# Seven block products instead of eight in the feed-forwards of a hybrid trunk

## The chip, the cores and the metric

The kernel runs on one core of a Trainium2 chip. The metric is the device time of one execution in microseconds (us), lower is better. The profiles are single executions taken by the hardware profiler; PE is the tensor engine, PEld its weight loads, DVE the vector engine, ACT the scalar engine, POOL the GpSimd engine, SP the queue that issues the transfers.

## The reference

A trunk of two layers over 512 latent tokens and 256 context tokens, model width 1024. Each layer is a half-step feed-forward, a mixing of the tokens by four groups of heads, and a second half-step feed-forward; every one of them starts from a modulated RMS norm. What matters here:

```python
def swiglu(h, w_in, w_out):            # w_in: 1024 x 5632, w_out: 2816 x 1024
    a, b = jnp.split(h @ w_in, 2, axis=-1)
    return (jax.nn.silu(a) * b) @ w_out

x = x + 0.5 * mx[2][:, None] * swiglu(modulate(x, ...), p['ffn_in'][0], p['ffn_out'][0])
# ... the mixers ...
x = x + 0.5 * mx[8][:, None] * swiglu(modulate(x, ...), p['ffn_in'][1], p['ffn_out'][1])
```

The context goes through the same weights, but not in the last feed-forward, whose result nobody reads.

## The kernel before

Everything is feature-major: features on the 128 partitions, tokens along the free axis (768, or 512 in the last feed-forward). The two streams are held side by side, so a feed-forward is one matrix product over 768 columns. There are four feed-forwards, called F1 to F4 here: F1 and F3 begin the two layers, F2 and F4 end them. F4 has 512 tokens, the others 768.

Products are kept near float32 accuracy by splitting each operand into a high part, rounded to the format that the tensor engine takes, and a low part, the rest (`split`, L72 to L78: ACT casts the high part at L77, DVE or POOL subtracts for the low part at L78). One product is then three matmuls: high by high, high by low, low by high.

`ffn` (L308) walks over 22 feature tiles in four parts (`PARTS`, 6, 6, 5 and 5 tiles). For a tile, `weights` loads 128 x 2048 weights (8 blocks of input features by 256 output features, the gate's 128 and the value's 128) and splits them; `x_ffn_in` makes the two products, for the first 512 tokens and then for the other 256 (two times 256 in F4), takes the silu of the first, multiplies, and splits the result into `g`. The first two tiles of a feed-forward are done together, segment by segment, since the second segment's norm is still under way. After a part, `out_product` multiplies the part's rows of the second weight matrix and adds to `X` (`resid`, L276). The last part's second product runs segment by segment (`out_and_norm`), so that the norm of the first segment runs beside the products of the second.

Work on the side: the modulation of later sub-layers (`mod_tile`, L179) is given to `ffn` as a list of calls, three or two for each tile. A modulation tile is one load of 512 KB and two multiply-and-accumulate operations of DVE over 128 x 1024 (L186). F1 has 56 of these tiles, F2 24, F3 48, F4 none.

The order of the work of each engine is not written by hand: a planner puts each instruction on its engine's queue by its own estimate of when it is ready, in the order of the program where several are. Each engine then runs its queue strictly in order.

Of the kernel before, what the change touches and what calls it, by code (L numbers as in the profile page):

```python
# [17 lines left out]
L = 2  # L18
# [6 lines left out]
PARTS = (6, 6, 5, 5)  # L25
# [3 lines left out]
# columns of the packed per-partition vectors  # L29
# [17 lines left out]
# feature tiles of the input projection: R = rwkv, then the others  # L47
# [5 lines left out]
class Net:  # L53
# [4 lines left out]
    # ---------------------------------------------------------------- small helpers  # L58
# [29 lines left out]
    def rsqrt(self, pool, val, n, cap=None, tag=""):  # L88
        """1/sqrt of [128, n] values in SBUF"""
# [15 lines left out]
    # ---------------------------------------------------------------- constants  # L105
# [20 lines left out]
    # ---------------------------------------------------------------- phase of dense layers  # L126
    def open_early(self, st):
        """what the output projection needs; attention still runs"""
# [3 lines left out]
        self.wp = p(name="wp", bufs=2)  # L132
# [19 lines left out]
    def weights(self, src, nk, w, pool=None, hi_eng=None):  # L152
        """load [128, nk, w] and split it"""
        pool = pool or self.wp
        raw = pool.tile([128, nk, w], F32, tag="wraw", name="wraw", bufs=2 if pool is self.wp else 3)
        hi = pool.tile([128, nk, w], F32R, tag="whi", name="whi")
        lo = pool.tile([128, nk, w], F32R, tag="wlo", name="wlo")
        self.load(raw, src)
        self.split(hi, lo, raw, None if pool is self.wp else self.nc.gpsimd, hi_eng)
        return hi, lo  # L160

    def product(self, w, sl, h, sg, nk):
        """rows sl of the weights times the tokens sg, in PSUM"""
        whi, wlo = w
# [3 lines left out]
        for k in range(nk):  # L168
            for i, (a, b) in enumerate(((whi, hi), (whi, lo), (wlo, hi))):
                self.mm(o, a[:, k, sl], b[k][:, sg], start=k == 0 and i == 0, stop=k == nk - 1 and i == 2)  # L170
# [8 lines left out]
    def mod_tile(self, l, j):  # L179
        """72 tiles of 128 modulation values, for both streams"""  # L180
# [8 lines left out]
    def mod_done(self, l, i, k=0, n=8):  # L189
        """the 9 groups of 8: shift, scale, gate of the three sub-layers"""  # L190
# [31 lines left out]
    def norm_squares(self, sg):  # L222
        """sums of squares of the tokens sg over the feature tiles"""
        nc = self.nc
        n = sg.stop - sg.start
        if self.hold:
            # in the room of the modulation's input: the next modulation begins after this norm's sums
            acc = self.mp.tile([128, 512], F32, tag="cb", name="acc", bufs=1)
        else:
            acc = self.ep.tile([128, 512], F32, tag="acc", name="acc", bufs=1)  # L230
# [11 lines left out]
    def norm_root(self, acc, n, bank):  # L242
        """1 / rms of n tokens, spread over the partitions"""
# [24 lines left out]
    def norm(self, l, n, sg, h):  # L268
        """modulated RMS norm of the tokens sg of X, as hi and lo parts"""
# [8 lines left out]

    def out_product(self, l, n, src, g, nk, segs, first=None):
        for jp in range(4):  # L280
            w = first if first and jp == 0 else self.weights(src[jp], nk, 256)
            for jj in range(2):
                for sg in segs:
# [1453 lines left out]
```

## Time and profile before

| | |
|---|---|
| time of the runs | 3416.62 us median of three (3416.52, 3416.62, 3434.64) |
| profiled execution, first to last instruction | 3425.9 us |
| PE busy | 3261.6 us (95%) |
| DVE busy | 1854.7 us (54%) |
| ACT busy | 1027.2 us (30%) |
| POOL busy | 387.3 us (11%) |
| granted TensorE clock, mean | 0.957 of full speed |

The profiled execution has no other time than its span, which lies within the spread of the runs. Busy time of PE counts matmuls whose recorded ends overlap the next one's start, so the pace of PE is read from the starts of successive matmuls.

### The profile page before, as it was taken

What the parts mean: (1) busy time and instruction counts of PE and PEld (TensorE: products, weight loads), DVE (VectorE), ACT (ScalarE), POOL (GpSimd) and SP (SyncE); (2) the same over time, 40 slices, a digit from 0 to 9 for tenths busy, and PEclk for the clock granted to TensorE, in tenths of its full rate; (3) what the DMA queues carried; (4) which work ended last, traced back from release to release, by engine and by line L of the source; (5) the groups of instructions that cost most, each with busy time, mean ns of one, the idle gap of its engine ahead of it and who ended that gap; (6) DMA issues with size and microseconds to landing.
All of it is one profiled execution on the core that took longest, in us unless ns stands there. A gap on an engine that the chain in (4) does not pass through costs nothing.

```text
span 3425.9 us, 53700 instructions
## 1 busy us (share of the span) xinstructions
PE 3261.6 (95%) x22388; PEld 2834.0 (83%) x22388; DVE 1854.7 (54%) x3491; ACT 1027.2 (30%) x1511; POOL 387.3 (11%) x416
## 2 busy tenths in 40 slices
PE   7999999899889988999999999999899879989999
PEld 6888888777778767888888888888777667689999
DVE  7994234567955358623235993332557955363333
ACT  4211212442233344121123312112443234352222
POOL 0001000234332100000000001000145332000000
PEclk9999999999889899999999999999999879989999
DMA  7662112223142114411112562221323231132223
GB/s 251 203 217 97 61 70 75 82 77 97 64 122 61 49 61 163 145 56 68 56 65 96 188 213 79 70 73 50 108 63 104 82 97 39 39 115 96 87 93 111
DMA packets 154756, 337.77 MB, mean 99 GB/s; under 512 B 60784, under 2 KB 81104, under 8 KB 142864
## 3 DMA queue, kind: packets, MB, share of 16 engines
q1 hardware_dynamic: 154512, 334.33, 30.1%
q8 instruction: 176, 2.88, 0.3%
q14 instruction: 68, 0.56, 0.1%
HBM read 307.09 MB, written 27.18 MB: 98 GB/s over the span
## 4 chain that ended last, share of the span: by engine, by line
PE 84%; DVE 8%; DMA 3%; ACT 2%; issue 1%; SPq 0%; POOL 0%; DVEq 0%; ACTq 0%; POOLq 0%
PE pt L63 60%; PE pj L63 8%; PE pr L63 6%; PE sc L63 3%; PE ps L63 2%; PE po L63 1%; PE pg L63 1%; PE pc L63 1%; DVE inv L1121 1%; DVE T L1119 1%; DVE junk L186 0%; ACT whi L77 0%; SPq L60 0%; ACT t L264 0%; DMA sg<-cd 0%
## 5 line engine op out<-in xcount | busy, mean ns | idle before, releaser
L63 PE MATMUL pt<-hh,whi 128*128 128x256 f32 (+1 forms) x2816 | 909.9, 327 | 28.9 <-ACT hh L77 26.6
L63 PE MATMUL pt<-hl,whi 128*128 128x256 f32 (+1 forms) x2816 | 915.5, 326 | 3.4 <-DVE hl L78 3.1
L63 PE MATMUL pt<-hh,wlo 128*128 128x256 f32 (+1 forms) x2816 | 911.1, 325 | 0.0
L63 PE MATMUL pt<-g,whi 128*128 128x256 f32 (+1 forms) x2816 | 642.6, 323 | 0.0
L77 ACT ACTIVATE whi<-wraw 128x2048 fp32r<-128x2048 f32 (+4 forms) x272 | 349.5, 1285 | 852.3 <-PE pt L63 569.0
L63 PEld LDWEIGHTS pt<-hh,whi 128*128 128x128 f32 x2816 | 539.3, 193 | 73.7 <-ACT hh L77 28.7
L63 PEld LDWEIGHTS pt<-hl,whi 128*128 128x128 f32 x2816 | 541.2, 192 | 49.0 <-DVE hl L78 6.9
L63 PEld LDWEIGHTS pt<-hh,wlo 128*128 128x128 f32 x2816 | 540.6, 192 | 42.6
L63 PEld LDWEIGHTS pt<-g,whi 128*128 128x128 f32 x2816 | 471.2, 190 | 42.1
L63 PE MATMUL pt<-g,wlo 128*128 128x256 f32 (+1 forms) x1408 | 451.4, 323 | 0.0
L78 DVE TENSOR_TENSOR wlo<-wraw,whi 128x2048 fp32r<-128x2048 f32 (+3 forms) x184 | 349.1, 1897 | 133.8 <-ACT whi L77 133.3
L305 DVE TENSOR_TENSOR sa<-sa,pt 128x256 f32<-128x256 f32 (+1 forms) x176 | 91.7, 521 | 577.9 <-PE pt L63 576.2
L186 DVE SCALAR_TENSOR_TENSOR junk<-wm,cb 128x1024 bf16<-128x1024 f32 x272 | 332.0, 1221 | 21.9 <-ACT cb L177 11.5
L276 DVE SCALAR_TENSOR_TENSOR X<-pt,hg,X 128x256 f32<-128x256 f32 (+1 forms) x288 | 165.7, 579 | 264.2 <-PE pt L63 263.6
L63 PEld LDWEIGHTS pt<-g,wlo 128*128 128x128 f32 x1408 | 266.4, 190 | 21.5
L78 POOL TENSOR_TENSOR wlo<-wraw,whi 128x512 fp32r<-128x512 f32 x88 | 128.7, 1465 | 892.3 <-ACT whi L77 883.0
L77 ACT ACTIVATE g<-sa 128x256 fp32r<-128x256 f32 (+1 forms) x176 | 86.1, 489 | 402.5 <-DVE sa L305 402.4
L63 PE MATMUL pj<-hh,whi 128*128 128x512 f32 x616 | 190.6, 374 | 11.2 <-DVE k L935 8.3
L304 ACT ACTIVATE sa<-pt 128x256 f32<-128x256 f32 (+1 forms) x176 | 81.7, 464 | 364.4 <-PE pt L63 364.4
L63 PE MATMUL pj<-hh,wlo 128*128 128x512 f32 x616 | 185.8, 369 | 0.0
L63 PE MATMUL pj<-hl,whi 128*128 128x512 f32 x616 | 185.4, 369 | 0.0
L75 POOL CAST wh<-gS 128x512 fp32r<-128x512 f32 x8 | 6.7, 844 | 1148.8 <-PE pt L63 870.8
(416 smaller groups left out, 3911.8 us busy)
## 6 DMA issues: line engine op xcount, KB each, us to landing
wraw<-in_ffn_in SPq DMA_DIRECT2D x88, 1024.0 KB, 4.9
wm<-in_w_mod SPq DMA_DIRECT2D x144, 512.0 KB, 3.7
wraw<-in_ffn_out SPq DMA_DIRECT2D x48, 640.0 KB, 3.9
wraw<-in_ffn_out SPq DMA_DIRECT2D x32, 768.0 KB, 4.3
wraw<-in_w_in SPq DMA_DIRECT2D x88, 256.0 KB, 2.6
wraw<-in_w_out SPq DMA_DIRECT2D x16, 512.0 KB, 3.7
xd<-X SPq DMA_DIRECT2D x16, 384.0 KB, 3.5
wa<-in_w_out SPq DMA_DIRECT2D x16, 256.0 KB, 3.1
```

The source lines that it names most:

```text
L63: self.nc.tensor.matmul(out, lhsT=lhsT, rhs=rhs, start=start, stop=stop, skip_group_check=skip)
L75: hi_eng.tensor_copy(hi, src)
L77: self.nc.scalar.activation(out=hi, in_=src, func=AF.Copy)
L78: (eng or self.nc.vector).tensor_tensor(lo, src, hi.bitcast(F32), op=ALU.subtract)
L186: nc.vector.scalar_tensor_tensor(out=junk, in0=w, scalar=1.0, in1=self.cb[:, s], op0=ALU.mult, op1=ALU.mult, accum_out=self.mod[l][:, s, j ...
L276: self.nc.vector.scalar_tensor_tensor(out=self.X[j][:, sg], in0=o, scalar=self.hg[l][:, s, 8 * n + j:8 * n + j + 1], in1=self.X[j][:, sg], ...
L304: nc.scalar.activation(out=sa, in_=a, func=AF.Silu)
L305: nc.vector.tensor_tensor(sa, sa, b, op=ALU.mult)
L1119: nc.vector.tensor_tensor(tv, N[:, s, tt].unsqueeze(2).to_broadcast([96, nt, nj]), X[:, s, jj].unsqueeze(1).to_broadcast([96, nt, nj]), op ...
L1121: nc.vector.tensor_tensor(X[:, tt, jj], X[:, tt, jj], tv, op=ALU.add)
```

## The change

The first product of a feed-forward is seen as a product of 2 x 2 blocks: the weights of two neighbouring tiles (rows) by the two halves of the 1024 input features, times the input `h` by the same halves of the features and the two halves of the tokens (384 and 384, or 256 and 256). Eight block products become seven, with sums of blocks of the weights before, sums of blocks of `h` before, and sums of the results after (Strassen's scheme in Winograd's order).

- The first pair of tiles of each feed-forward is still done the old way (`ffn_tiles`), since the tokens' norm is still under way. Then `token_sums` makes the sums of blocks of `h`, in `T1`, `T2`, `T4` and, over a part of `h`, `T3`. The other ten pairs go through `ffn_seven`, once for the gate and once for the value.
- For a pair and one of gate and value, `ffn_seven` makes four weight sums on POOL (128 x 512), seven operand splits (ACT and DVE, 128 x 512), seven products of 12 matmuls over half the tokens, two copies of PSUM on ACT, four additions on DVE and one on POOL. The last of the seven is issued after the first of the next group.
- Six parts of 4, 4, 4, 4, 4 and 2 tiles; the second product works by 128 output features a load, not 256, and in F4 over all 512 tokens at once, but for the last part.
- The pools are cut anew: three split operands in spare rooms (`SPARE`), five operand buffers of 4 blocks, two modulation buffers in place of three; the weights lie in DRAM in the order in which they are now read.

```diff
-PARTS = (6, 6, 5, 5)
+PARTS = (4, 4, 4, 4, 4, 2)
...
-        self.mp = self.pools(self.mod_room, "right")(name="mp", bufs=3)
+        self.mp = self.pools(self.mod_room, "right")(name="mp", bufs=2)
...
+    def token_sums(self, h, nt):
...
+        T = {n: [self.tp.tile([128, 4, NT // 2], F32R, tag=f"T{n}{q}", name="T") for q in range(2)] for n in (1, 2, 4)}
...
+        for k in range(4):
...
+            sub(v, t1, h12, h11)
+            add(v, t1, t1, l12)
+            sub(v, t1, t1, l11)
+            sub(v, t2, h22, t1)
+            add(v, t2, t2, l22)
+            self.split(T[2][0][:, k, :m], T[2][1][:, k, :m], t2)
+            self.split(T[1][0][:, k, :m], T[1][1][:, k, :m], t1)
+            sub(g, t3, h22, h12)
+            add(g, t3, t3, l22)
+            sub(g, t3, t3, l12)
+            sub(g, t4, h21, t2)
+            add(g, t4, t4, l21)
+            self.split(T[4][0][:, k, :m], T[4][1][:, k, :m], t4, g)
+            self.split(hi[k][:, b], lo[k][:, b], t3, g)
...
+    def ffn_seven(self, l, f, i0, g, gi, B, nt):
...
+        def done(ab, at, src):
+
+            t, sl = where[at]
+            if ab == 0:
+                gate[at] = self.ep.tile([128, 512], F32, tag="e", name="gate")[:, :m]
+                nc.scalar.activation(out=gate[at], in_=src, func=AF.Silu)
+                return
+            nc.vector.tensor_tensor(gate[at], gate[at], src, op=ALU.mult)
+            self.split(g[0][gi + t][:, sl], g[1][gi + t][:, sl], gate[at])
+
+        def mult(o, op, p, first, last):
+            hi, lo = B[p]
+            for k in range(4):
+                for i, (x, y) in enumerate(((op[0], hi), (op[0], lo), (op[1], hi))):
+                    self.mm(o, x[:, k], y[k], first and k == 0 and i == 0, last and k == 3 and i == 2, skip=True)
+
+        for ab in range(2):
+            r0, r1 = [self.raw(self.A["ffn_in"][l, f, i0 + i, ab], KD) for i in range(2)]
+            a11, a12, a21, a22 = r0[:, 0:4], r0[:, 4:8], r1[:, 0:4], r1[:, 4:8]
+            S = lambda: self.wp.tile([128, 4, 128], F32, tag="ws", name="ws", bufs=3)
+            p1, p6, p5 = bank(), bank(), bank()
+            mult(p1, self.operand(a11), 1, True, True)
+            s1 = c("s1")
+            self.copy(s1, p1)
+            if self.defer:
+                self.defer.pop()()
+            w1, w2 = S(), S()
+            nc.gpsimd.tensor_tensor(w1, a21, a22, op=ALU.add)
+            nc.gpsimd.tensor_tensor(w2, w1, a11, op=ALU.subtract)
+            mult(p6, self.operand(w2), 6, True, True)
+            u2 = c("u2")
+            nc.vector.tensor_tensor(u2, s1, p6, op=ALU.add)
+            mult(p5, self.operand(w1), 5, True, True)
+            s5 = c("s5")
+            self.copy(s5, p5)
+            mult(p1, self.operand(a12), 2, False, True)
+            done(ab, "11", p1)
+            w3 = S()
+            nc.gpsimd.tensor_tensor(w3, a11, a21, op=ALU.subtract)
+            mult(p6, self.operand(w3), 7, False, True)
+            u3 = c("u3")
+            nc.vector.tensor_tensor(u3, s1, p6, op=ALU.add)
+            nc.gpsimd.tensor_tensor(s5, s5, u3, op=ALU.add)
+            done(ab, "22", s5)
+            w4 = S()
+            nc.gpsimd.tensor_tensor(w4, a12, w2, op=ALU.subtract)
+            mult(p5, self.operand(w4), 3, False, True)
+            nc.vector.tensor_tensor(u2, u2, p5, op=ALU.add)
+            done(ab, "12", u2)
+
+            def last(ab=ab, p6=p6, s1=s1, op=self.operand(a22)):
+                mult(p6, op, 4, False, True)
+                nc.vector.tensor_tensor(s1, s1, p6, op=ALU.add)
+                done(ab, "21", s1)
+
+            self.defer.append(last)
...
-            for i0 in ([0, 2, 3, 4, 5] if part == 0 else range(np_)):
...
+            for i in range(0, np_, 2):
...
+                if B is None:
+                    self.ffn_tiles(l, f, m0, g, h, segs)
+                    B = self.token_sums(h, nt)
+                else:
+                    self.ffn_seven(l, f, m0 + i, g, i, B, nt)
+                for _ in range(2 * per):
                     if side:
                         side.pop(0)()
...
-            if part < 3:
-                self.out_product(l, n, src, g, np_, segs)
+            if part < len(PARTS) - 1:
+                self.out_product(l, n, src, g, np_, segs if nt == NT else [slice(0, nt)])
```

## Rows read from the trace of the kernel before

**Rows 1.** The page: busy time of each engine, and the last chain by engine.

```profile
PE 3261.6 (95%) x22388; PEld 2834.0 (83%) x22388; DVE 1854.7 (54%) x3491; ACT 1027.2 (30%) x1511; POOL 387.3 (11%) x416
...
PE 84%; DVE 8%; DMA 3%; ACT 2%; issue 1%; SPq 0%; POOL 0%; DVEq 0%; ACTq 0%; POOLq 0%
```

**Rows 2.** Busy time by stretch: length, each engine's, granted clock, DMA share, GB/s.

```profile
155.00:205.00 50.00, 50.00 (x289) 44.24 (x288) 47.18 (x78) 6.63 (x6) 0.00 (x0) 1.00 0.66 217
...
480.00:563.00 83.00, 83.00 (x480) 73.59 (x479) 20.75 (x24) 17.93 (x25) 0.00 (x0) 1.00 0.15 50
...
1861.00:1910.00 49.00, 40.48 (x208) 34.54 (x208) 37.73 (x81) 28.52 (x50) 0.00 (x0) 0.90 0.33 108
...
3146.00:3215.00 69.00, 69.00 (x578) 69.00 (x576) 22.53 (x29) 19.58 (x30) 0.00 (x0) 1.00 0.23 81
```

**Rows 3.** PE's order of time, F1's fourth part: first and last of 28.

```profile
499.79 0.39 PE L63 MATMUL pt<-hl,whi 128*128 128x512 f32 x1
...
505.91 0.39 PE L63 MATMUL pt<-hl,whi 128*128 128x512 f32 x1
```

**Rows 4.** PE's order of time, F4's second part: first and last of 19.

```profile
3149.84 0.28 PE L63 MATMUL pt<-hl,whi 128*128 128x256 f32 x1
...
3152.00 0.28 PE L63 MATMUL pt<-hl,whi 128*128 128x256 f32 x1
```

**Rows 5.** Groups by shape on POOL: count, busy us, mean ns, idle before.

```profile
L78 POOL TENSOR_TENSOR wlo<-wraw,whi 128x512 fp32r<-128x512 f32 x88 | 128.7, 1465 | 892.3 <-ACT whi L77 883.0 <-ACT gqk L524 6.9 <-DVE ls L604 1.2
...
L655 POOL TENSOR_TENSOR a<-am 128x256 f32<-128x256 f32 x20 | 14.8, 744 | 33.4 <-DVE am L653 24.6 <-PE ps L63 7.1 <-DVE s_te L815 1.7
...
L823 POOL TENSOR_TENSOR sg<-s_dt,cst 128x384 f32<-128x384 f32 x8 | 8.0, 1018 | 1.9 <-DVE sg L828 1.7
```

**Rows 6.** DVE's order of time at the start of F3.

```profile
1866.86 1.28 DVE L78 TENSOR_TENSOR hl<-t,hh 128x512 fp32r<-128x512 f32 x2
...
1890.17 1.23 DVE L186 SCALAR_TENSOR_TENSOR junk<-wm,cb 128x1024 bf16<-128x1024 f32 x1 [4.41 <-ACT cb L177]
...
1891.44 1.23 DVE L186 SCALAR_TENSOR_TENSOR junk<-wm,cb 128x1024 bf16<-128x1024 f32 x1
...
1892.59 1.41 DVE L263 TENSOR_TENSOR t<-X,ps 128x256 f32<-128x256 f32 x4
```

**Rows 7.** The modulation's line L186 by stretch of F1: DVE busy, clock, DMA share, GB/s.

```profile
87.00:155.00 68.00, 45.58 (x75) 1.00 0.66 212
155.00:205.00 50.00, 31.79 (x53) 1.00 0.66 217
205.00:265.00 60.00, 42.80 (x69) 1.00 0.65 209
265.00:355.00 90.00, 5.14 (x10) 1.00 0.25 84
```

**Rows 8.** POOL and DVE beside each other, in order of time, after F1.

```profile
613.14 1.30 POOL L78 TENSOR_TENSOR wlo<-wraw,whi 128x512 fp32r<-128x512 f32 x1
...
613.40 1.58 DVE L78 TENSOR_TENSOR hl<-t,hh 128x512 fp32r<-128x512 f32 x1 [0.66 <-ACT hh L77]
...
614.40 1.75 POOL L78 TENSOR_TENSOR wlo<-wraw,whi 128x512 fp32r<-128x512 f32 x1
...
615.02 0.69 DVE L263 TENSOR_TENSOR t<-X,ps 128x512 f32<-128x512 f32 x1
```

**Rows 9.** End of F2 and first pair of F3, in order of time.

```profile
1845.14 0.39 PE L63 MATMUL pt<-g,wlo 128*128 128x512 f32 x1
...
1866.20 2.08 PE L63 MATMUL pt<-hh,whi 128*128 128x512 f32 x4 [4.52 <-ACT hh L77]
...
1903.59 0.75 DVE L78 TENSOR_TENSOR hl<-t,hh 128x256 fp32r<-128x256 f32 x2
...
1909.55 0.28 PE L63 MATMUL pt<-hh,wlo 128*128 128x256 f32 x1
```

**Rows 10.** The first 5.7 us of F3 by stretch, columns as in rows 2.

```profile
1866.20:1871.90 5.70, 5.70 (x13) 4.46 (x14) 5.70 (x10) 5.27 (x9) 0.00 (x0) 0.50 0.53 187
```

More of the change, by code (lines that the diff above doesn't have):

```diff
@@ L277, in resid, with out_weights @@
                                             in1=self.X[j][:, sg], op0=ALU.mult, op1=ALU.add)
+    def out_weights(self, src, nk):
+        return [self.operand(self.raw(src, nk)[:, :nk], nk)]
     def out_product(self, l, n, src, g, nk, segs, first=None):
[L280 to L283, printed above, removed]
-                    o = self.product(w, slice(128 * jj, 128 * jj + 128), g, sg, nk)
-                    self.resid(l, n, 2 * jp + jj, o, sg)
+        for j in range(KD):
+            ws = first if first and j == 0 else self.out_weights(src(j), nk)
+            for sg in segs:
+                self.resid(l, n, j, self.product(ws, g, sg, nk), sg)
     def out_and_norm(self, l, n, src, g, nk, nt, nxt, first=None):
@@ L298, in out_and_norm, with ffn_tiles @@
         return h
-    def x_ffn_in(self, g, i, w, h, sg):
+    SPARE = ((("gp", "gh2", 1), ("gp", "gl2", 1)), (("gp", "gh3", 1), ("gp", "gl3", 1)), (("wp", "ws", 3), ("wp", "ws", 3)))
+    def ffn_tiles(self, l, f, i0, g, h, segs):
         nc = self.nc
-        a, b = [self.product(w, slice(128 * half, 128 * half + 128), h, sg, KD) for half in range(2)]
-        sa = self.ep.tile([128, 512], F32, tag="e", name="sa")[:, :sg.stop - sg.start]
-        nc.scalar.activation(out=sa, in_=a, func=AF.Silu)
-        nc.vector.tensor_tensor(sa, sa, b, op=ALU.mult)
-        self.split(g[0][i][:, sg], g[1][i][:, sg], sa)
+        ws = {}
+        n = 0
+        for i in range(2):
+            for ab in range(2):
+                raw = self.raw(self.A["ffn_in"][l, f, i0 + i, ab], KD)
+                sets = []
+                for q in range(2):
+                    room = [(getattr(self, p), t, b) for p, t, b in self.SPARE[n - 5]] if n >= 5 else None
+                    sets.append(self.operand(raw[:, 4 * q:4 * q + 4], 4, room))
+                    n += 1
+                ws[i, ab] = sets
+        for sg in segs:
+            for i in range(2):
+                a, b = [self.product(ws[i, ab], h, sg, KD) for ab in range(2)]
+                sa = self.ep.tile([128, 512], F32, tag="e", name="sa")[:, :sg.stop - sg.start]
+                nc.scalar.activation(out=sa, in_=a, func=AF.Silu)
+                nc.vector.tensor_tensor(sa, sa, b, op=ALU.mult)
+                self.split(g[0][i][:, sg], g[1][i][:, sg], sa)
@@ new lines, in ffn_seven @@
+    def ffn_seven(self, l, f, i0, g, gi, B, nt):
+        nc = self.nc
+        m = nt // 2
+        a, b = slice(0, m), slice(m, nt)
+        c = lambda n: self.ep.tile([128, NT // 2], F32, tag="c", name=n, bufs=8)[:, :m]
+        bank = lambda: self.pj.tile([128, 512], F32, tag="pj", name="pt")[:, :m]
+        where = {"11": (0, a), "12": (0, b), "21": (1, a), "22": (1, b)}
+        gate = {}
+        def done(ab, at, src):
[11 more added lines that the diff above has]
+                    self.mm(o, x[:, k], y[k], first and k == 0 and i == 0, last and k == 3 and i == 2, skip=True)
+        for ab in range(2):
+            r0, r1 = [self.raw(self.A["ffn_in"][l, f, i0 + i, ab], KD) for i in range(2)]
[35 more added lines that the diff above has]
+            self.defer.append(last)
@@ L333, in ffn @@
             side.pop(0)()
+        room.close()
         if nxt and nxt[1] == 1:
```

85 lines of the change are left out of this document (56 added, 29 removed).

## The prediction

> **What bounds the kernel now.** I read the page first: PE is busy for 95% of the span and makes 84% of the chain that ended last [rows 1]. Busy shares are averages, so I read the stretches next: inside the feed-forwards PE is busy in every microsecond at full granted clock, whether DVE is nearly full (47.2 of 50 us, F1) or three quarters idle (20.8 of 83 us), and POOL does nothing at all there [rows 2]. Only at the seams does PE wait, as between F2 and F3, where it is busy for 40.5 of 49 us [rows 2]. So a feed-forward lasts as long as its matmuls, and the pace of one is read from starts: (505.91 - 499.79) / 27 = 0.2267 us at 512 columns [rows 3] and (3152.00 - 3149.84) / 18 = 0.1200 us at 256 [rows 4]. The difference is 1/2.4 ns a column, plus 13 ns a matmul. For 384 columns, which do not occur, I take 0.1733 us by that line.
>
> **What it removes.** A pair of tiles over 768 tokens has 96 matmuls of 512 columns and 96 of 256: 33.28 us. After it has 2 x 7 x 12 = 168 of 384: 29.11 us. With 512 tokens, 192 of 256 (23.04 us) become 168 (20.16 us). Ten pairs in each feed-forward change: 30 x 4.17 + 10 x 2.88 = 154 us. F4's second product turns 480 pairs of 256 (115.2 us) into 480 of 512 (108.8 us): 6 us. In all 160 us less of PE.
>
> **What it adds in a pair.** Durations first. DVE operations of one kind follow each other at 1.28 - 0.68 = 0.60 us for 512 columns, (1.41 - 0.41) / 3 = 0.33 for 256, thus 0.465 for 384, and 1.27 for one half of a modulation tile [rows 6]. POOL takes 1.30 us for 512 columns when nothing disturbs it [rows 8], some 0.74 for 256 and 1.0 for 384 [rows 5]. For a pair over 768 tokens DVE then has 14 operand splits (8.4 us), 8 additions from PSUM and 4 multiplications and 4 splits of the gate (16 x 0.465 = 7.4): 15.9 us. POOL has 8 weight sums and 2 additions: 12.4 us. ACT has 14 casts and 12 smaller operations, near 14 us. All three fit under 29.1 us of PE if they run side by side. That is the question, because POOL was idle here before.
>
> They don't quite run side by side. At 613.40 a DVE subtraction with both inputs in SBUF starts behind a POOL one, lasts 1.58 us and ends 0.55 us after POOL's end (614.44); the next POOL operation then lasts 1.75 us, waiting for it; a DVE operation with one input in PSUM keeps its 0.69 us beside POOL [rows 8]. So I count DVE operations with two SBUF inputs and POOL's as taking turns. The Trainium skill speaks against this change here: its page "SBUF — State Buffer", section "Who interferes with whom", says that a DVE instruction with two SBUF inputs contends with a GpSimd instruction that reads SBUF, and that the later one waits for the whole of the other. The rows above agree; taken alone, by that rule the work of a pair would be a sum where a reader of busy shares sees a maximum.
>
> Two-input work of DVE in a pair: 14 splits and 7 of the 16 others, 8.4 + 3.3 = 11.7 us.
>
> - **Pairs without modulation, 768 tokens.** 11.7 + 12.4 = 24.1 us in turn, 28.3 even if the PSUM reads queue too: under 29.1. Cost 0; at most 2 us a pair, 16 pairs, 32 us, for waits in an order planned without turns.
> - **Pairs with modulation beside them.** The planner runs modulation as early as DVE has room: DVE stays 94% full [rows 2] until the tiles are used up near 265 us [rows 7]. After the change it will fill the same 94% of 29.1 us: 27.4 - 15.9 = 11.5 us, 4.5 tiles a pair, and some 7 in a part's second product (33 us of PE, 14 of DVE). Behind the first pair F1 has 207 / 4 = 52 tiles left, each being four entries [rows 7], which reach over 6 pairs and the second products between them; by the same share F3's 45 reach over 5 pairs and F2's 22 over 3: 14 pairs. There turns need 11.7 + 11.5 + 12.4 = 35.6 us against 29.1; with the shorter stay of a held operation (0.55 for 0.60 us) 33.6. I take 34.5: 5.4 x 14 = 75 us. Bounds: 0 if the planner's order happens to fit, 39.8 a pair (150 us) if the PSUM reads queue as well.
> - **Pairs of F4.** DVE's two-input work is 8.4 + 7 x 0.33 = 10.7 us, POOL's 8 x 1.3 + 2 x 0.74 = 11.9: 22.6 in turn against 20.2 of PE, 25.6 with all. I take 22: 18 us; bounds 0 and 54. Hence F4's pairs gain next to nothing over 23.04.
>
> **The sums of tokens.** They cannot start before the norm of the last tokens, and the third product needs them. In F3 the last low part is written at 1904.3 and the first pair's last matmul starts at 1909.55 [rows 9]: PE has 5.5 us left, then four products of the gate that need little of them (8.3 us) and two of the value (4.2): 18 us. The sums need 28 DVE operations (13.0 us), 28 of POOL (28 us), and POOL's first three weight sums (3.9): 45 us in turn, from some 4 us before the norm's end (an estimate: a block needs one tile of each half of the features). So PE waits 41 - 18 = 23 us if they take turns, 28 + 3.9 - 4 - 18 = 10 if POOL alone counts. I take 18, nearer to the turns since both engines have nothing else but two-input work here. In F4 the same sum with 256 columns gives 6 to 16; I take 12. Together 66 us (36 to 85).
>
> **What comes with it.** After an idle stretch PE runs at half the granted clock: 13 matmuls in 5.7 us at 0.50 [rows 10], 2.6 us lost. Four new waits: 10 us. The last part has two tiles, not five, so the second segment's products that hide the norm shrink from 120 x 0.12 = 14.4 to 5.8 us. Before, 21 us passed from the first segment's last matmul to the first of the next feed-forward, 4.5 of them idle [rows 9]. Part of those 21 us was DVE at work for the second segment, which shrinks too; I take 4 of the 8.6 us at three seams: 12 us (0 to 26). The mixers' first weights, prepared on POOL in mid-F1 before, must now wait until the `T` tiles are done with; some 14 us of POOL behind 17 us of second product: 0, up to 10 if that cover is gone. Loads are smaller and more, of the same bytes at a DMA share of 0.15 to 0.66 [rows 2]: 0. Five additions into `X` instead of three lie behind matmuls of the second product: 0.
>
> **The sum.** 3425.9 - 160 + 75 + 0 + 18 + 66 + 10 + 12 = 3447 us for the profiled execution, which is 9.3 us above the median of the runs. Against that median: 3438 us.
>
> By the skill's rule named above to the letter, pairs with modulation take 35.6 us, F4's 22.6 and the sums of tokens 85 in all: 91 + 24 + 85 + 10 + 12 - 160 = +62, or 3479 us; no run shows yet how a long row of such operations shares its time, so I stay below it.
>
> **Rivals.**
> - *The work hides* (chance 0.32). The turns cost nothing in the pairs and only POOL's own time shows at the sums of tokens: -160 + 36 + 10 + 12 = -102, 3315 us; anything up to 3395 counts here. For it: PE did not wait while DVE was 94% full [rows 2], and operands are split five ahead. Against it: that DVE had no neighbour on POOL.
> - *All in turn* (0.18). Beyond two-input operations, PSUM reads queue behind held operations, since DVE runs in order: 150 for the pairs with modulation, 54 in F4, 85 for the sums, 10 and 12: 311 - 160 = +151, 3568 us. It decides for slower by much once a pair with modulation lasts over 36 us. For it: the held operation of rows 8. Against it: DVE keeps 0.69 us beside POOL in the same rows.
> - *Results leave PSUM too late* (0.05). A product that adds to a bank waits until the bank was read; two products (4.2 us) lie between. A modulation half (1.27), a POOL operation (1.3), a held split (0.55) and the read (0.47) are 3.6 us, just under. From 4.2 on each pair would pay: 2 us in each of 60 halves is +120 on my sum, 3558 us.
> - *Fewer columns, no less time* (0.03). If a matmul of 384 columns took the 0.2267 us of 512, a pair would need 38.1 us and the sum would be near 3600. Rows 3 and 4 lie on one line with the clock's slope, which speaks against it.
>
> **How the numbers follow.** The likeliest case (0.42) is the sum above: the saving is eaten up by the turns and by the sums of tokens. Its own range, 3395 to 3480, comes from about half of each bound. A change of 0.5% (17 us) is what a measurement of this kernel can tell. Of the 0.42, 0.04 lies below 3400, 0.18 within 3400 to 3434, 0.20 above. Faster: 0.32 + 0.04 = 0.36; same 0.18; slower 0.20 + 0.18 + 0.05 + 0.03 = 0.46. For 8 in 10 the range leaves out the low end of the first rival (about 0.09) and the high end of the others (about 0.1): 3325 to 3535 us.
>
> **What would show it.** Matmuls of 384 columns start 0.173 us apart, and a pair without modulation lasts 29 us with PE unbroken; at 33 the first step is wrong. In F1 and F3 pairs beside L186 last 33.5 to 36 us, DVE's 128 x 512 splits grow from 0.69 to over 1 us and POOL's weight sums over 1.3; at 30 the turns were overrated. Between the first pair and the first product with `T` PE waits 10 to 23 us in F1 to F3, at half clock after. The wait at the seams grows from 4.5 to some 8 us. The prediction fails most easily at the number of modulation tiles that the planner puts beside a pair, and at how much of the sums of tokens it finds room for ahead of the norm's end.

## The result and the profile after

The changed kernel takes 3570.6 us (median of four, 3564.3 to 3577.5) against 3422.3: a ratio of 1.0418, 95% interval 1.0383 to 1.0452. It is slower by 148 us, where the prediction had 3438 us and a range up to 3535. The profiled execution has a span of 3573.3 us against 3425.9, 147.4 more. The page, busy time by engine and the last chain by engine:

```profile
PE 3188.3 (89%) x20948; PEld 2815.7 (79%) x20948; DVE 2525.0 (71%) x4675; ACT 1314.2 (37%) x2399; POOL 1118.2 (31%) x928
...
PE 65%; DVE 23%; DMA 5%; issue 4%; ACT 2%; POOL 1%; SPq 1%; DVEq 0%; ACTq 0%; POOLq 0%
```

PE has less to do, and its share of the chain falls from 84% [rows 1] to 65%; DVE's rises from 8% to 23%. Where that is shows in the windows by stretch (length, busy time of each engine, granted clock, DMA share, GB/s): F2 behind its first pair, a pair of F1 beside modulation with the pair after it, two pairs of F2 with their second product, the same in F4, and the seam between F2 and F3.

```profile
1404.00:1456.00 52.00, 12.85 (x30) 6.50 (x29) 52.00 (x63) 10.94 (x23) 37.76 (x25) 0.54 0.25 80
218.00:280.00 62.00, 57.29 (x317) 55.98 (x317) 62.00 (x96) 22.19 (x43) 22.42 (x14) 0.97 0.44 140
1612.00:1704.00 92.00, 92.00 (x533) 88.05 (x532) 53.44 (x84) 32.83 (x60) 27.55 (x20) 1.00 0.23 70
3278.00:3342.00 64.00, 62.62 (x437) 58.55 (x436) 48.38 (x76) 29.43 (x61) 26.17 (x21) 1.00 0.31 100
1930.00:1980.00 50.00, 33.98 (x154) 27.94 (x152) 34.20 (x85) 22.06 (x41) 1.26 (x1) 0.83 0.31 111
```

The middle of F2 is as forecast, with PE unbroken. The first row is the loss: for 52 us DVE is busy in every one of them, and PE does 30 matmuls, at a mean granted clock of 0.54. Three such stretches stand in the trace, one behind the first pair of each of F1, F2 and F3. What DVE and POOL do in the middle of this one (order of time: start, duration, engine and line):

```profile
1421.82 2.29 DVE L200 SCALAR_TENSOR_TENSOR junk<-wm,cb 128x1024 bf16<-128x1024 f32 x1
1424.03 0.08 DVE L200 DVE_READ_ACCUMULATOR junk<-wm,cb 128x1 f32 x1
1424.03 0.55 DVE L355 TENSOR_TENSOR t<-t,hl 128x384 f32<-128x384 f32 x1
1424.50 0.68 DVE L78 TENSOR_TENSOR wlo<-ws,whi 128x512 fp32r<-128x512 f32 x1
1425.11 2.02 DVE L200 SCALAR_TENSOR_TENSOR junk<-wm,cb 128x1024 bf16<-128x1024 f32 x1
1427.05 0.08 DVE L200 DVE_READ_ACCUMULATOR junk<-wm,cb 128x1 f32 x1
1427.05 1.60 DVE L354 TENSOR_TENSOR t<-hh 128x384 f32<-128x384 f32 x1
1428.58 1.34 DVE L78 TENSOR_TENSOR T<-t,T 128x384 fp32r<-128x384 f32 x1
1429.84 1.21 DVE L200 SCALAR_TENSOR_TENSOR junk<-wm,cb 128x1024 bf16<-128x1024 f32 x1
```

```profile
1421.56 1.46 POOL L414 TENSOR_TENSOR ws<-ws,wraw 128x512 f32<-128x512 f32 x1 [0.68 <-POOL ws L413]
1424.66 1.38 POOL L354 TENSOR_TENSOR t<-hh,t 128x384 f32<-128x384 f32 x1 [1.64 <-DVE t L355]
1426.00 2.24 POOL L424 TENSOR_TENSOR ws<-wraw 128x512 f32<-128x512 f32 x1
1428.20 1.30 POOL L355 TENSOR_TENSOR t<-t,hl 128x384 f32<-128x384 f32 x1
```

L200 is the modulation (L186 before). The planner put halves of modulation tiles between the sums of tokens, 15 in these 52 us. Some of them wait for POOL and make POOL wait: 7 of the 15 lasted over 1.5 us. From F2's first product to its second part there are 47 halves, with a mean of 1458 ns, where one alone lasts 1.23 us [rows 6].

### The profile page after: what moved, and what is told of

Same layout as the page of the kernel before. It is cut to its first block, busy times and chain, and to the rows that moved or that the text cites. A ratio compares the mean times of both kernels' runs of the same rounds, so it can differ in the third digit from the quotient of the medians.

```text
span 3573.3 us, 55156 instructions
## 1 busy us (share of the span) xinstructions
PE 3188.3 (89%) x20948; PEld 2815.7 (79%) x20948; DVE 2525.0 (71%) x4675; ACT 1314.2 (37%) x2399; POOL 1118.2 (31%) x928
## 4 chain that ended last, share of the span: by engine, by line
PE 65%; DVE 23%; DMA 5%; issue 4%; ACT 2%; POOL 1%; SPq 1%; DVEq 0%; ACTq 0%; POOLq 0%
PE pt L63 41%; PE pj L63 7%; PE pr L63 6%; DVE junk L200 6%; DVE wlo L78 3%; PE sc L63 3%; PE ps L63 2%; PE po L63 1%; PE pc L63 1%; PE pg L63 1%; DVE t L354 1%; DMA wm<-in_w_mod 1%; DVE g L78 1%; DVE T L1261 1%; DVE inv L1263 1%
## 5 line engine op out<-in xcount | busy, mean ns | idle before, releaser
L63 PE MATMUL pt<-g,whi 128*128 128x512 f32 (+1 forms) x2496 | 633.3, 344 | 13.4 <-ACT g L77 5.9
L77 ACT ACTIVATE whi<-wraw 128x512 fp32r<-128x512 f32 (+1 forms) x616 | 366.6, 605 | 669.2 <-PE pt L63 409.4
L63 PE MATMUL pt<-T,whi 128*128 128x384 f32 (+1 forms) x1920 | 470.3, 331 | 111.2 <-ACT T L77 42.5
L63 PE MATMUL pt<-hh,whi 128*128 128x384 f32 (+2 forms) x1536 | 500.5, 337 | 48.0 <-DVE u L417 25.7
L63 PE MATMUL pt<-hl,whi 128*128 128x384 f32 (+2 forms) x1536 | 508.7, 333 | 7.0 <-DVE hl L78 7.0
L63 PE MATMUL pt<-hh,wlo 128*128 128x384 f32 (+2 forms) x1536 | 504.9, 332 | 9.1 <-DVE wlo L78 9.1
L78 DVE TENSOR_TENSOR wlo<-wraw,whi 128x512 fp32r<-128x512 f32 (+1 forms) x528 | 407.9, 779 | 79.0 <-ACT whi L77 74.6
L63 PEld LDWEIGHTS pt<-T,whi 128*128 128x128 f32 x1920 | 339.4, 192 | 127.4 <-ACT T L77 49.6
L63 PE MATMUL pt<-g,wlo 128*128 128x512 f32 (+1 forms) x1248 | 422.6, 344 | 2.5 <-DVE wlo L78 2.5
L200 DVE SCALAR_TENSOR_TENSOR junk<-wm,cb 128x1024 bf16<-128x1024 f32 x272 | 380.3, 1398 | 17.6 <-ACT cb L191 10.1
L63 PE MATMUL pt<-T,wlo 128*128 128x384 f32 (+1 forms) x960 | 313.3, 328 | 12.8 <-DVE wlo L78 12.7
```

Source lines behind the costliest of these rows:

```text
L63: self.nc.tensor.matmul(out, lhsT=lhsT, rhs=rhs, start=start, stop=stop, skip_group_check=skip)
L200: nc.vector.scalar_tensor_tensor(out=junk, in0=w, scalar=1.0, in1=self.cb[:, s], op0=ALU.mult, op1=ALU.mult, accum_out=self.mod[l][:, s, j ...
```

## Where the 147 us are, by the terms of the prediction

The stretches come from starts and ends of matmuls in the profiled executions. "Old product, six parts" is an experiment below: the kernel before with the new `PARTS` alone, which serves as the base for each part.

| term | predicted | measured | how |
|---|---|---|---|
| less PE | -160 | -160 | 91.8 us for two pairs and a second product against 100.1 in the old product |
| starts: sums of tokens and half clock | +76 | +183 | first product to second part, F1 209.6 (from the span's start), F2 164.2, F3 164.0, F4 91.7, against 156.7, 113.7, 113.0, 78.2 with the old product, which less one pair's saving (4.2, in F4 2.9) leaves 57 + 55 + 55 + 16 |
| pairs beside modulation | +75 | +38 | four stretches of two pairs and a second product, 101.1, 103.1, 101.5 and 98.8, against 91.7 |
| pairs of F4 | +18 | +7 | four stretches, 255.6 in all, against 4 x 62.1 of matmuls |
| seams, mixers, parts | +12 | +79 | the rest; F1's end to F2, F2's to F3 and F3's to F4 are 1355.9 us together against 1298.3, 58 of it; 14 is what six parts cost inside the old product's feed-forwards; some 7 were not traced |

## The experiments

Twelve further kernels ran. The table has for each its ratio to the kernel before on the same chip with its 95% interval, the span of its profile, what its four starts take over those of the old product less the saving (183 in the changed kernel; kernels whose first part has two tiles are measured to the third part, against the old product with the same parts), and what the two mixers and the seam between F2 and F3 take over the 1298.3 us of before. The last three columns come from one execution each, and the runs of one kernel lie 4 to 28 us apart, so differences of a few us say nothing.

| kernel | ratio | span | starts | mixers and seam |
|---|---|---|---|---|
| changed kernel | 1.0418 (1.0383 to 1.0452) | 3573.3 | +183 | +58 |
| modulation after the sums | 1.0238 (1.0208 to 1.0268) | 3510.2 | +99 | +59 |
| no modulation | 1.0032 (1.0014 to 1.0050) | 3438.3 | +86 | +59 |
| no token sums | 0.9961 (0.9947 to 0.9974) | 3412.1 | +17 | +53 |
| token sums on DVE | 1.0336 (1.0311 to 1.0361) | 3535.1 | +145 | +55 |
| no POOL | 1.0172 (1.0146 to 1.0199) | 3484.8 | +132 | +67 |
| first part of two tiles | 1.0258 (1.0231 to 1.0286) | 3506.5 | +155 | +27 |
| no POOL, first part of two | 0.9962 (0.9944 to 0.9981) | 3417.2 | +96 | +31 |
| modulation after, first part of two | 1.0058 (1.0036 to 1.0081) | 3453.1 | +86 | +21 |
| all three | 0.9859 (0.9837 to 0.9882) | 3387.5 | +46 | +52 |
| old product, six parts | 1.0181 (1.0144 to 1.0217) | 3471.0 | 0 | +31 |
| old product, first part of two | 1.0096 (1.0074 to 1.0119) | 3472.1 | 0 | +26 |
| old product, two modulation buffers | 1.0079 (1.0052 to 1.0107) | 3449.4 | as before | +16 |

**Theories.** A: the starts lose their time to modulation that the planner weaves between the sums. B: the turns of DVE and POOL set it, and modulation only fills gaps. C: the shorter last part uncovers the norms. The first four kernels tell A from B; those with the old product test C.

### Modulation after the sums

```diff
                     B = self.token_sums(h, nt)
+                    if side:
+                        last = B[4][1][3].bitcast(F32)[:, 0:1].unsqueeze(1).to_broadcast([128, 2, 1])
+                        self.nc.vector.scalar_tensor_tensor(out=self.cb[:, :, 0:1], in0=last, scalar=0.0, in1=self.cb[:, :, 0:1],
+                                                            op0=ALU.mult, op1=ALU.add)
```

> F1 to F3 differ from the changed kernel in one thing: an operation that reads the last sum of tokens writes a column of the modulation's input, so no modulation tile of the feed-forward can start before the sums are done. Theory A (modulation between the sums: in the changed kernel 27 modulation halves, 40.3 us of DVE, lie in the 80 us behind F2's first pair) expects the stretch from a feed-forward's first product to its first product with the second matrix to fall from 134 us in F2 and F3 to about 102 (62.4 of matmuls and 40 of waits, the 29 that F4 shows without modulation times 1.4 for its columns), and some 9 more pairs to take 34.5 us: 3 x 32 - 9 x 5.4 = 47 us, thus about 3520 us. Theory B (the turns of DVE and POOL inside the sums set their time, and the modulation only fills the gaps) expects 128 us or more for the stretch and 3570 to 3610 us in all, since the modulation comes on top later.

3508.9 us, 62 less, and from F2's first product to its second part 129.3 us instead of 164.2. That is 35 us less; up to the first product with the second matrix, theory A asked for 32 and theory B for 6 at most. DVE's modulation in these two stretches, the changed kernel first, then here:

```profile
L200 DVE SCALAR_TENSOR_TENSOR junk<-wm,cb 128x1024 bf16<-128x1024 f32 x47 | 68.5, 1458 | 5.8 <-ACT cb L191 5.7
```

```profile
L200 DVE SCALAR_TENSOR_TENSOR junk<-wm,cb 128x1024 bf16<-128x1024 f32 x18 | 24.1, 1337 | 0.4 <-DMA wm<-in_w_mod 0.3
```

PE's waits for the sums of tokens (`T`) in the same order (time in all, number, longest):

```profile
PE pt L63 <- ACT T L77: 15.1, 5, 5.2
PE pt L63 <- DVE T L78: 15.0, 5, 4.4
```

```profile
PE pt L63 <- DVE T L78: 5.0, 3, 2.9
...
PE pt L63 <- ACT T L77: 3.8, 2, 3.0
```

They fall from 30 to 9 us. The feed-forwards alone gain 65 us here. The moved modulation makes more pairs slow (the second part of F2 now takes 102.3 us instead of 91.8): the pairs cost 20 us more in all, where 49 was expected.

### No modulation, and no token sums

```diff
-            for j in range(8 * i, 8 * i + 8):
-                calls.append(lambda j=j: self.mod_tile(l, j))
+            calls.append(lambda i=i: self.nc.vector.memset(self.mod[l][:, :, 8 * i:8 * i + 8], 0.01))
```

> The modulation tiles on the side of F1 to F3 (loads and DVE operations) are left out; a constant stands in their place. Theory A expects the stretches at the starts of F2 and F3 at about 102 us instead of 134, every pair at 29 to 30 us and the total at 3570 - 3 x 32 - 8 x 5.4 = 3430 us. Theory B expects the starts at 125 us or more, and 3500 us. If pairs without modulation still lasted 32 us or more, the turns would cost there too.

3440.1 us, and the starts still take 86 us more than the old product's: in F2 and F3 21 each, in F4 18. That is the price of the sums by themselves, and it is the 76 us that the prediction had for sums and half clock, within 10. All pairs behind the starts of F1 to F3 last as long as their matmuls, so turns cost nothing in a pair of 768 tokens without modulation. (F4's pairs, shorter, cost 0.9 us each even without it.)

```diff
-                    B = self.token_sums(h, nt)
+                    B = self.token_blocks(h, nt)
```

> The sums of tokens are left out: the seven products take blocks of h itself, so the matmuls are as many and as long, on other numbers. All theories in which the starts carry the loss expect F2 and F3 to reach the second matrix in 66 us and F4 in 46, 3 x 68 + 27 = 230 us less there; the modulation done meanwhile (13 tiles each) moves to 9 other pairs at 5.4: 3570 - 230 + 49 = 3390 us. If the loss sat in the pairs instead, it would stay above 3500 us.

3411.9 us; the starts fall to +17, and the loss goes with them. It stays above the 3390 expected because the starts give back 166 us, not 230; the 230 was more than the 183 that they had lost. The modulation that had been done at the starts now stands beside twelve pairs, not eight, which cost 58 us, 20 more than in the changed kernel, where 49 more was expected.

### Token sums on DVE, and no POOL

```diff
-            v, g = nc.vector, nc.gpsimd
+            v, g = nc.vector, nc.vector
```

> The half of the token sums that POOL made goes to DVE; nothing else differs from the changed kernel. Theory A1 (the planner puts modulation only where DVE waits for POOL) expects few modulation halves between the sums: 56 operations of 0.55 us are 31 us of DVE, so that from F2's first product to the first product of its second part it takes 125 to 130 us instead of 164 (130 without modulation), and with the modulation moved to some 9 pairs at 5.4 the total is 3570 - 2 x 36 - 20 + 49 = 3527 us. Theory A2 (the planner weaves modulation into the sums anyhow, since both are ready) expects 150 to 160 us for that stretch and 3550 to 3570 us in all.

3539.0 us, 153.3 us for F2's stretch. The stretch is that of theory A2; the total lies between the 3527 of A1 and the 3550 to 3570 of A2. With POOL's half of the sums gone, the modulation is woven in all the same. DVE in order of time in the same place:

```profile
1432.04 1.21 DVE L200 SCALAR_TENSOR_TENSOR junk<-wm,cb 128x1024 bf16<-128x1024 f32 x1
1433.19 0.08 DVE L200 DVE_READ_ACCUMULATOR junk<-wm,cb 128x1 f32 x1
1433.19 0.55 DVE L354 TENSOR_TENSOR t<-hh,t 128x384 f32<-128x384 f32 x1
1433.66 0.55 DVE L354 TENSOR_TENSOR t<-hh 128x384 f32<-128x384 f32 x1
1434.13 0.55 DVE L354 TENSOR_TENSOR t<-t,hl 128x384 f32<-128x384 f32 x1
1434.60 0.55 DVE L78 TENSOR_TENSOR T<-t,T 128x384 fp32r<-128x384 f32 x1
1435.06 1.21 DVE L200 SCALAR_TENSOR_TENSOR junk<-wm,cb 128x1024 bf16<-128x1024 f32 x1
```

In these lines each sum takes 0.55 us and each half 1.21, where both were up to a microsecond longer beside POOL; the order is as bad. POOL still makes weight sums at the starts, so not all turns are gone. Taking the sums of tokens from POOL gives 38 us at the starts (theory B), taking all its work there 51 (the next kernel), and holding the modulation back 84 (theory A).

For the second kernel of this pair the weight sums and the addition into `s5` go to DVE as well:

```diff
-            nc.gpsimd.tensor_tensor(w1, a21, a22, op=ALU.add)
+            nc.vector.tensor_tensor(w1, a21, a22, op=ALU.add)
...
-            nc.gpsimd.tensor_tensor(s5, s5, u3, op=ALU.add)
+            nc.vector.tensor_tensor(s5, s5, u3, op=ALU.add)
```

> Token sums, weight sums and the one addition of POOL all go to DVE: POOL does nothing in the feed-forwards' products. The theory of turns expects the pairs beside modulation back at 29 to 30 us (35 in the changed kernel, 8 pairs), since DVE's 21.4 us of own work a pair leave room for three tiles of modulation: 45 us less than the same kernel with only the token sums on DVE, 3480 us. A rival, that DVE is then full and becomes the bound, expects pairs of 32 us or more over more pairs, since the modulation lasts longer, and 3527 us or more; in F4, where a pair has 20.2 us of PE and DVE about 20, it expects pairs of 21 to 23 us.

3482.9 us. Two pairs beside modulation and their second product take 91.9 us (F1, 191.2 to 283.1), no more than without modulation, and in F4 62.0 us, the time of the matmuls. DVE is nearly full there and PE does not wait; the window over this stretch:

```profile
191.00:284.00 93.00, 93.00 (x537) 89.02 (x537) 89.48 (x163) 33.05 (x61) 0.00 (x0) 1.00 0.43 147
```

That DVE becomes the bound in the pairs is refuted: the five stretches with 20 to 27 modulation halves take 91.9 to 92.4 us (101.1 to 103.1 with 35 in three of the changed kernel, 98.8 with 13 in the fourth). So the turns were nearly the whole price of the pairs beside modulation. What they cost an operation is read from DVE's groups by shape, the changed kernel first, then this one:

```profile
L200 DVE SCALAR_TENSOR_TENSOR junk<-wm,cb 128x1024 bf16<-128x1024 f32 x272 | 380.3, 1398 | 17.6 <-ACT cb L191 10.1 <-DMA wm<-in_w_mod 6.8
L78 DVE TENSOR_TENSOR wlo<-wraw,whi 128x512 fp32r<-128x512 f32 x464 | 378.0, 822 | 73.7 <-ACT whi L77 69.5
```

```profile
L200 DVE SCALAR_TENSOR_TENSOR junk<-wm,cb 128x1024 bf16<-128x1024 f32 x272 | 333.4, 1226 | 17.0 <-ACT cb L191 10.0 <-DMA wm<-in_w_mod 6.7
L78 DVE TENSOR_TENSOR wlo<-wraw,whi 128x512 fp32r<-128x512 f32 x464 | 316.8, 690 | 48.2 <-ACT whi L77 42.4
```

The same split takes 822 ns with POOL's sums and 690 without. A 128x512 weight sum, which POOL made in some 1500 ns, takes DVE 689. In all DVE took over work for which POOL had been busy 730 us (1118.2 less 388.5) and was itself busy for 2546.3 us instead of 2525.0.

### The parts

```diff
-PARTS = (6, 6, 5, 5)
+PARTS = (4, 4, 4, 4, 4, 2)
...
-            for i0 in ([0, 2, 3, 4, 5] if part == 0 else range(np_)):
+            for i0 in ([0, 2, 3] if part == 0 else range(np_)):
```

> The kernel before with six parts of 4, 4, 4, 4, 4 and 2 tiles, and nothing else of the change. Theory C (the shorter last part uncovers the norms): the waits behind F1, F2, F3 and the first half of a layer's output grow as in the changed kernel, by 8 + 13 + 9 us, and with the end of the mixers' longer part about 3425 + 30 + (0 to 30): 3455 to 3485 us. If the parts cost nothing it is 3417 to 3430 us, and the mixers' loss belongs to the pools or to POOL's work. The wait between the output projection and F2 (6 us longer in the changed kernel) should not change here, since no part is involved.

3483.5 us, at the top of theory C's bounds; in the profile 45 us more, of which 31 lie in the mixers and the seam and 14 in the feed-forwards. But the seam between F2 and F3 grew by 3.3 us only (7.8 against 4.5), where theory C had 13. The wait between the output projection and F2 stays at 5.4 us, as expected. To tell the short last part from the number of parts, the old product ran with two tiles first:

```diff
-PARTS = (6, 6, 5, 5)
+PARTS = (2, 4, 4, 4, 4, 4)
```

> The kernel before with parts of 2, 4, 4, 4, 4 and 4 tiles (in F1 the gate's nine calls come right behind the first pair). It splits the cost of six parts (45 us in the profiles with the short part last) by its cause. If the short last part costs it, because the norm of the first tokens has too little beside it, some 10 to 20 us over the kernel before are left, 3435 to 3445 us. If it is the number of parts, or the order in which the planner then lays out the mixers, 3460 us or more.

3465.7 us, 33 more than the kernel before on the same chip, where the forecasts, made from 3425, were 10 to 20 and 35 or more. By the runs about half of the cost of six parts goes with the short last part (a ratio of 1.0096 against 1.0181, with intervals that don't meet), and half stays. The profiles show the same time for both (3472.1 and 3471.0 us), but the profiled execution was the slowest of its kernel here and the fastest there. The seam of F2 and F3 is nearly back (5.5 us, before 4.5), and the two mixers still take 25 us more. Their code is the same in all kernels. The last run therefore changes something that the mixers don't use at all:

```diff
-        self.mp = self.pools(self.mod_room, "right")(name="mp", bufs=3)
+        self.mp = self.pools(self.mod_room, "right")(name="mp", bufs=2)
```

> The kernel before with two modulation buffers in place of three, one small part of the change that no line of the mixers uses. In the eleven kernels run so far, from F1's last matmul to F2's first took 701 to 733 us (692 before) and from F3's last to F4's first 606 to 632 (605 before), with the mixers' code the same in all. Theory E (the planner lays out the mixers anew from where each engine stands at the end of the feed-forward, and its order before was a good one) expects the sum of the two to move by 10 us or more here too, and the total by as much, with the feed-forwards within 3 us. The rival, that the loss there comes from the changed parts, weights and rooms themselves, expects both stretches within 3 us of before.

3450.2 us, 0.8% slower (0.5 to 1.1). The profile has 23.5 us more: 6.6 up to F1's end (theory E had 3 at most), 1.3 or less in each other feed-forward, and 16.3 in the mixers, 10.2 of them in the first and 6.1 in the second. The mixers' work is equal by the page:

```profile
PE 3282.4 (95%) x22388; PEld 2849.9 (83%) x22388; DVE 1855.5 (54%) x3491; ACT 1027.9 (30%) x1511; POOL 386.3 (11%) x416
```

The counts of PE, DVE, ACT and POOL are those of [rows 1]. So a loss of this size in the mixers needs no cause in their work. The planner's order differs, on DVE most of all, and the place of their rooms in memory may. In the first of the two mixers the same matmuls kept PE busy for 649.1 us instead of 635.1, at a granted clock of 0.88 instead of 0.90. Which of order and place it is was not tried.

### A longer last part, and the three together

The next kernels have parts of 2, 4, 4, 4, 4 and 4 tiles, so that the first pair's second product stands between the first pair and the third product.

```diff
-PARTS = (4, 4, 4, 4, 4, 2)
+PARTS = (2, 4, 4, 4, 4, 4)
...
+                    if (l, f) == (0, 0):
+                        for _ in range(9):
+                            side.pop(0)()
                     B = self.token_sums(h, nt)
```

> The changed kernel with parts of 2, 4, 4, 4, 4 and 4 tiles; in F1 the nine calls that make the gate of the residual come ahead of the token sums, since the first second product needs it. Two effects are expected: the last part is long again, so that of the 45 us that six parts cost with the old product (profiles: 3471.0 against 3425.9) some 35 come back; and the first pair's second product, 16 us of PE (11 in F4), lies between the first pair and the third product and covers that much of the token sums in each feed-forward, 55 to 60 us if modulation still lies between the sums. Together 3570 - 95 = 3475 us. If the cost of six parts comes from their number and not from the short last one, 3510 us; if the second product is issued behind the third product's wait and so covers nothing, 3535 us.

3512.3 us, not 3475. The mixers and the seam gave back 31 us, but the starts only 28 instead of 55 to 60: with the modulation woven in, DVE is late by more than the 16 us of second product. PE still waits 23 us for `T` in F2, and the second product waits for DVE too: in F2 for splits of its operands (9 us), in F1 30 us for residuals.

> Both of the last two together: no POOL in the feed-forwards' products, parts of 2, 4, 4, 4, 4 and 4 tiles. If the causes add up, 3480 - 35 for the long last part - 4 x 8 to 15 for the token sums that the first second product covers = 3385 to 3415 us, under the kernel before. If DVE becomes the bound, 3440 us or more.

3414.8 us, at the upper bound: by 0.4% under the kernel before.

> The changed kernel with parts of 2, 4, 4, 4, 4 and 4 tiles and the modulation of F1 to F3 held until the last token sum (in F1 the gate's nine calls ahead of the sums); POOL keeps its work. The two effects act on the same stretch, so they don't add in full: held modulation leaves 17 to 19 us of wait for the sums, and the first second product covers 16 of them. First products to third pair in F2 as the best order would have it, 155 to 160 us; 9 more pairs beside modulation at 4.7. From 3512 (two first): 3 x 32 less, 42 more: 3458 us. If the sums' turns with POOL take longer when weight sums of the next part queue behind them, 3480 us or more.

3451.6 us, 6 under the sum, though its terms came out otherwise: F2's first product to its third part takes 174.5 us, where 155 to 160 was expected and the old product took 166.2. With POOL's turns it takes 66.1 us until the second part begins (58.1 in the kernel below), since the first second product waits for DVE; and the third part, beside modulation, takes 101.2 us against 91.8.

> No POOL in the feed-forwards' products, parts of 2, 4, 4, 4, 4 and 4 tiles, modulation of F1 to F3 held until the last token sum. In the kernel with the first two of these, the starts of F2 and F3 still take 36 us more than their matmuls, with 23 us of PE idle in a row and modulation between the sums. If modulation between the sums is the cause, and a pair without POOL has room for modulation at no cost, both go: 3415 - 3 x 30 = 3325 us, 3 per cent under the kernel before. If instead DVE's 56 sums are late on their own account (31 us behind the norm, where PE has 34 of work), 3380 us; if the modulation no longer finds room in F1 and runs out over its end, 3360.

3387.6 us, 1.4% under the kernel before (1.2 to 1.6), the version that beats both kernels by most. The starts of F2 and F3 are 7.5 and 11.5 us over the old product's less the saving. Of the 62 us missing to 3325, F1's start makes 28: it was counted at 30 and gave 2. PE waits there for the gate of the residual (`hg`), which the second product of a first part of two tiles needs early and which DVE makes among modulation and sums. This wait is 25 to 30 us in all four kernels with seven products and two tiles first, so it was there already in the kernel that 3325 was worked out from. The mixers and the seam make 21: 52 us over before, against 31 in that kernel. PE's wait behind F1's first pair, DVE where it ends, and F2's start in the windows:

```profile
PE pt L63 <- DVE X L290: 25.0, 1, 25.0
```

```profile
125.54 0.17 DVE L216 TENSOR_SCALAR hg<-mod 128x16 f32<-128x16 f32 x1
...
126.08 3.24 DVE L290 SCALAR_TENSOR_TENSOR X<-pt,hg,X 128x512 f32<-128x512 f32 x6
```

```profile
1378.00:1448.00 70.00, 59.77 (x317) 57.15 (x317) 68.53 (x129) 30.16 (x59) 0.00 (x0) 0.93 0.30 96
```

The four feed-forwards are 90 us shorter than before in this kernel, and the mixers and the seam take back 52. The four kernels with two tiles first also show how the two causes share the starts (155, 96, 86 and 46 us): taking POOL out gives 59 us with the modulation woven in and 40 with it held back; holding it back gives 69 and 50.

## Why the prediction was wrong

**Right: what is removed.** Matmuls of 384 columns follow each other as read off the line through 256 and 512 columns. PE in order of time, F2:

```profile
1659.69 0.51 PE L63 MATMUL pt<-T,whi 128*128 128x384 f32 x2
...
1662.29 0.34 PE L63 MATMUL pt<-hh,whi 128*128 128x384 f32 x1
```

Fifteen starts lie between these two rows: 2.60 / 15 = 0.1733 us, the value taken. Two pairs and a second product lost 8.3 us, as 2 x 4.17 says. The rival "fewer columns, no less time" is out.

**Right in kind, too large in number: the turns in the pairs.** A pair beside modulation costs 4.7 us (37.7 over eight) where 5.4 was taken. But behind the starts only eight pairs had modulation beside them, not fourteen, since F2 for one had spent 47 of its 48 modulation halves at its start; three more pairs had it within the starts, and what they cost is part of the 183. F4's pairs cost 0.9 us each, not 1.8.

**The step that failed: the sums of tokens.** The prediction put PE's wait at 18 us "since both engines have nothing else but two-input work here". They had something else. It had itself noted that the planner runs modulation "as early as DVE has room", and then counted the modulation only "behind the first pair", in the seven-product pairs. The sums alone cost what it said (86 us with the half clock, 76 predicted). With modulation beside them they cost 183: after a first wait of 3.4 us the matmuls with `T` came one by one over 48 us (F2, 1407.9 to 1455.4), where one wait of 10 to 23 us was looked for. Holding it back brings 84 of those 97 us back, taking POOL out of the sums 38.

**The second step that failed: what comes with it.** Seams and mixers were put at 12 us, worked out from the second segment's products. The parts alone cost 45 us with the old product in the profiles (1.8% by the runs), and the mixers and the seam cost 58 us in the changed kernel. Part of it is the norm that lost its cover: at F2's end DVE's last sum of squares stands in a queue behind operand splits for the next feed-forward, which the planner put first. DVE in order of time, and PE's waits there:

```profile
1938.49 0.69 DVE L249 TENSOR_TENSOR acc<-acc,sq 128x512 f32<-128x512 f32 x1
1939.10 2.49 DVE L78 TENSOR_TENSOR wlo<-wraw,whi 128x512 fp32r<-128x512 f32 x4
1941.50 0.69 DVE L249 TENSOR_TENSOR acc<-acc,sq 128x512 f32<-128x512 f32 x1
1942.11 1.29 DVE L78 TENSOR_TENSOR wlo<-wraw,whi 128x512 fp32r<-128x512 f32 x2
1943.31 0.69 DVE L249 TENSOR_TENSOR acc<-acc,sq 128x512 f32<-128x512 f32 x1
```

```profile
PE ps L63 <- DVE acc L249: 8.6, 1, 8.6
PE pt L63 <- ACT hh L77: 2.9, 1, 2.9
PE ps L63 <- DVE rs_r L100: 2.5, 1, 2.5
```

These 14 us answer to the 4.5 of [rows 9]. With four tiles in the last part the seam takes 9.2 to 10.4 us, with two 17.1 to 17.8 (seven products). Most of the rest is within the mixers. One change that touches nothing of the mixers' work cost 16 us there; that the rest comes in the same way is not shown, and how it divides is open.

The errors of the four terms are +107 for the starts, +67 for seams and mixers, -37 for the pairs and -11 for F4: 126 us, the distance of the 3573 measured from the 3447 of the sum. The first two alone would have put it 174 us off; the pairs, priced too high, hid part of that.

**The rivals.** "The work hides" was wrong for DVE and POOL together and right for DVE alone: without POOL the pairs cost next to nothing. "All in turn" gave 3568 us, within 3 of the runs, but by luck: of its terms 150 for the pairs was 38, 54 for F4's was 7, 95 for the sums and the clock was 183, and 12 for the seams 79. A pair beside modulation lasted 33.8 us, under the 36 by which it wanted to be judged.

"Results leave PSUM too late" had all pairs pay, which they don't: PE is unbroken in pairs of 768 tokens without modulation. But where a pair pays, its wait is the main one: PE waits for `u` (L417), DVE's read of the bank to which the next product adds. It is 16.0 of PE's 25.6 us of waits in the four stretches beside modulation, and all of them in F4's. PE's waits on it in the two stretches of F1, the two of F3 and the four of F4:

```profile
PE pt L63 <- DVE u L417: 7.0, 2, 3.8
...
PE pt L63 <- DVE u L417: 9.0, 5, 3.0
...
PE pt L63 <- DVE u L417: 6.1, 4, 1.9
```

In the kernel without POOL, PE's only wait in the first two stretches of F1 beside modulation is this:

```profile
PE pt L63 <- ACT s L666: 0.3, 1, 0.3
```

So the turns make DVE late, and PE feels it mostly at this read, as "all in turn" had it for reads that queue behind held operations.

**The rule of the skill.** The Trainium skill ("SBUF — State Buffer", section "Who interferes with whom") says that a DVE operation with two inputs in SBUF contends with a POOL operation that reads SBUF, and that the later of the two waits for the whole of the other. The modulation half that starts at 1421.82 finds 1.20 us of POOL's operation (1421.56 + 1.46) still to go; with its own 1.22 that is 2.42 us, and it took 2.29. The trace agrees to 0.13 us. Where the rule to the letter gave 35.6 us for a pair beside modulation, 33.8 was measured.

## What to carry to other kernels

When work on the side has no due time of its own, count it into every stretch in which its engine is the one that the critical engine waits for, not only where the engine has room; and tie it to the end of that stretch by data. Before giving an idle engine work that takes operands from the same memory, work out what the busy engine would take for it: here 0.69 us against 1.5, and no turns. And before pricing a change by its stages, measure how much the untouched stages move under a planner when something small changes: here 16 us in the mixers, 0.5%, for one small change.

## What was not expected of the hardware

- The turns were forecast, their size was not: a modulation half held by POOL reached 2.29 us against 1.22 undisturbed, and POOL's 128x512 sum 2.24 us behind one. From 1424.66 to 1429.84 three operations of POOL and three of DVE follow each other in 5.2 us; undisturbed they take an estimated 5.6 in turn (1.0 + 1.3 + 1.0 by [rows 5] and [rows 8], and 1.22 + 2 x 0.55) and 3.3 side by side.
- With DVE busy for 89.5 of 93 us and POOL doing nothing, PE lost nothing over two pairs beside modulation; with DVE at 62.0 of 62 and POOL at 22.4 it was busy for 57.3 of 62 only.
